# A decoder trunk in split fp32: weight chunks that restart at each output projection, and dummy matmuls at the program's head

## The chip, the cores and the metric

The kernel runs on one core of a Trainium2 chip. Its time is the device time of one execution in microseconds (us): the median of several executions. A core has five engines that each take their instructions strictly in order: TensorE (PE; its weight loads are listed as PEld), VectorE (DVE), ScalarE (ACT), GpSimd (POOL) and SyncE (SP, which here only issues DMAs). An engine waits at an instruction until the semaphores that it needs are set; what stands behind it on the same engine waits too.

## The reference

Two layers work on x, 256 tokens by 2048, all in fp32. In each layer three groups of attention heads share one normalised input; then follows a gated MLP with a short causal convolution.

```
for l in range(DEPTH):                       # DEPTH = 2
    h = _rmsnorm(x, attn_norm[l])
    z = einsum('bsd,de->bse', h, w_in[l])    # 2048 -> 4934, split into q, k, v ... of three kinds of heads
    ...
    x = x + einsum('bsm,md->bsd', mix, w_o[l])           # output projection, 2048 -> 2048
    h = _rmsnorm(x, ffn_norm[l])
    u = conv3(einsum('bsd,df->bsf', h, w_up)) + conv_b   # 2048 -> 2 x 5632, three taps along the tokens
    a, g = split(u, 2)
    x = x + einsum('bsf,fd->bsd', silu(g) * a, w_down)   # 5632 -> 2048
return _rmsnorm(x, final_norm)
```

## The kernel before, in words

**Split arithmetic.** Each fp32 weight block of 128x128 is split on the chip into a high part (`hi`, a cast on ACT, L134) and the rest (`lo`, a subtract on DVE, L135). An activation tile `h` holds its own high and low part side by side, 2 x 256 tokens. A product is hi times both parts (512 columns, L189) plus lo times the high part (256 columns, L194).

**The weight stream.** All weights lie in HBM as one stream of blocks in the order in which PE reads them. SP loads them in chunks of `CH` = 16 blocks, 1 MB, into three `raw` buffers (`load`, L105). `convert` splits a chunk in pieces of `SUB` = 8 blocks: one cast and one subtract of 128x1024 each, into five `hi` and five `lo` buffers. `weights(b)` is asked for each block in turn; at the first block of a piece it converts that piece and the two behind it, and loads the next two chunks. So the place of the casts and subtracts among the other work follows from where a piece begins.

**Where pieces begin.** A layer's stream has 708 blocks up to the output projection and 2368 from there (output projection and MLP). Before, chunks are counted over the whole stream. 708 is 44 x 16 + 4, so in layer 0 everything from the output projection on lies 4 blocks, half a piece, off the pieces, and so does layer 1's attention; in layer 1 the second 708 makes it 8, a whole piece, and its output projection and MLP lie on whole pieces.

**Tiles.** `mm_t` makes one tile of 128 outputs out of 16 blocks: two whole pieces, or three pieces with a half at each end. Tiles alternate in order (`turn_of`): one has its 16 high matmuls (L189), then its 16 low ones (L194); the next has one high, 16 low, 15 high. `mm_t2` (L225 to L228) makes the first two tiles of a stage together, step by step of the inner loop, and `mm_first` (L207 to L211) the next; `mm_v` (L243 to L245) serves the output and down projections.

**The MLP.** A half of it makes 22 pairs of tiles, then a down projection with them. The first pair is an `mm_t2`, and 21 pairs of `mm_t` follow in the first half, 22 in the second. Each tile leaves its PSUM bank (there are three, tag `mm`) through `total`: an ACT copy of the upper half (L252) and a DVE sum (L254). Then POOL multiplies by the row norm (L817), ACT takes the tap with the bias (L820), DVE the two other taps (L821, L822). For the second tile of a pair ACT computes the Silu (L824), POOL the product (L825), and ACT and DVE the high and low part of the result (L503, L504).

**What sets the order.** The program is written in the order of the loops, with other work in background generators; a scheduler of the Tile framework then fixes each engine's order when the program is built. Nothing is decided on the chip.

**Start and end.** Before the first weights arrive, 18 dummy matmuls of 128x512 on a zeroed tile `heat` (L272) are issued into a bank that nobody reads; in the built program they stand in the middle of the first `mm_t2`, after ten of the 16 steps of its inner loop. `warm` is a small tile of zeros; in the last down projection, `gain(2)` (L844) calls `activation(warm, warm, Sqrt)`, and after the last matmul `norm.cols` (L434 to L436) takes the final root.

Of the kernel before, what the change touches and what calls it, by code (L numbers as in the profile page):

```python
# [15 lines left out]
P = 128  # L16
D = 2048
T = 256
KT = D // P
# [35 lines left out]
BIG = _split12(2.0 * math.pi * 4096.0, 4)  # L55


@with_exitstack
def kernel(ctx: ExitStack, tc: tile.TileContext, xin, xnat, pos, wstream, cst, par, fin, out):
    nc = tc.nc  # L60
# [29 lines left out]
    def f(ap):  # L90
        return ap.bitcast(F32)

    nblk = wstream.shape[0]
    wflat = wstream.rearrange("b p f -> (b p f)")
    nch = (nblk + CH - 1) // CH
    raws, subs = {}, {}
    bounds = [(i, min(SUB, nblk - i)) for i in range(0, nblk, SUB)]
    sub_of = {b: s for s, (at, n) in enumerate(bounds) for b in range(at, at + n)}

    def load(c):  # L100
        if c >= nch or c in raws:
            return
        n = min(CH, nblk - c * CH)
        t = wpool.tile([P, CH * P], F32, tag="raw", name=nm("raw"), bufs=3)
        nc.sync.dma_start(  # L105
            t[:, : n * P], wflat[c * CH * P * P : (c * CH + n) * P * P].rearrange("(p e) -> p e", p=P)
        )
        raws[c] = t

    def load_first():  # L110
# [10 lines left out]
    def convert(s, between=None):  # L121
        if s >= len(bounds) or s in subs:
            return
        at, n = bounds[s]
        c = at // CH
        load(c)
        o = (at - c * CH) * P
        src = raws[c][:, o : o + n * P]
        hi = wpool.tile([P, SUB * P], F32R, tag="hi", name=nm("hi"), bufs=5)
        lo = wpool.tile([P, SUB * P], F32R, tag="lo", name=nm("lo"), bufs=5)  # L130
        step = SUB // 2 * P if c < 3 else SUB * P
        for o in range(0, n * P, step):
            a = slice(o, min(o + step, n * P))
            nc.scalar.copy(hi[:, a], src[:, a])  # L134
            nc.vector.tensor_tensor(lo[:, a], src[:, a], f(hi[:, a]), ALU.subtract)  # L135
            if between is not None:
                between()
        subs[s] = (hi, lo)

    def weights(b, n=1):  # L140
        s = sub_of[b]
        at = bounds[s][0]
        if b == at:
            convert(s)
            convert(s + 1)
            convert(s + 2)
            load(b // CH + 1)
            load(b // CH + 2)
        o = (b - at) * P
        hi, lo = subs[s]  # L150
        return hi[:, o : o + n * P], lo[:, o : o + n * P]

# [107 lines left out]
    xr = [big.tile([P, D], F32, tag=f"x{t}", name=f"x{t}") for t in range(2)]  # L260
    xg = [slot().rearrange("p (j t) -> p j t", j=2) for k in range(KT // 2)]
    xT = [xg[k // 2][:, k % 2] for k in range(KT)]
    warm = small(4)
    nc.vector.memset(warm, 0.0)
    nc.scalar.activation(warm, warm, AF.Square)
    nc.scalar.dma_start(pr[0][:, :Q_CV], par[0, :, :Q_CV])
    load_first()
    heat = slot(F32R)
    nc.vector.memset(f(heat), 0.0)
    hot = bank("pv", 1)  # L270
    for i in range(18):
        nc.tensor.matmul(hot, heat[:, :P], heat, start=(i == 0), stop=(i == 17))  # L272
    nc.sync.dma_start(cs, cst)
    nc.sync.dma_start(pint, pos)
    nc.sync.dma_start(pr[0][:, Q_CV:], par[0, :, Q_CV:])
# [283 lines left out]
    for l in range(DEPTH):  # L559
# [244 lines left out]
        for half in range(2):  # L804
# [30 lines left out]
            else:  # L835
# [5 lines left out]
                def gain(j):  # L841
                    a = slice(j * 512, (j + 1) * 512)
                    if j == 2:
                        nc.scalar.activation(warm, warm, AF.Sqrt)  # L844
                    for t in range(2):
                        nc.gpsimd.tensor_tensor(xr[t][:, a], xr[t][:, a], gf[j], ALU.mult)

# [20 lines left out]
def _layout(inputs):  # L868
# [62 lines left out]
    flat = stream.reshape(-1)  # L931
    pend = np.concatenate(blocks)
    del blocks[:]
    for c in range(0, nblk, CH):
        n = min(CH, nblk - c)
        flat[c * P * P : (c + n) * P * P].reshape(P, n, P)[:] = pend[c : c + n].transpose(1, 0, 2)
    del pend

# [59 lines left out]
```

## Time and profile before

| | |
|---|---|
| median of 3 runs | 2303.63 us (2303.62 to 2304.62) |
| profiled execution | 2304.31 us, of it 2302.5 in the span of the trace |
| PE busy | 2246.5 us, 98% of the span, 12090 matmuls |
| DVE busy | 1472.0 us, 64% |
| ACT busy | 1205.4 us, 52% |
| POOL busy | 414.5 us, 18% |
| L135 subtracts | 775, 950.3 us, mean 1235 ns |
| L134 casts | 775, 803.9 us, mean 1040 ns |
| HBM traffic | 413.59 MB, 180 GB/s |
| chain that ended last | PE 78%, DVE 11%, ACT 5%, POOL 4%, issue 2% |

How to read it: shares of busy time are averages over the whole program. The span is what lies between the first and the last instruction of the profiled execution; the time has 1.8 us more. The chain follows the work back from the last instruction to what released each step: PE holds 78% of it, so for the rest of the time some other engine was what PE waited for, or what stood at the two ends. Which stage that is, the tables by stretch and the waits of PE tell.

### The profile page before, as it was taken

How to read it: one execution, taken by the hardware profiler on the slowest of the kernel's cores; microseconds unless marked ns; L12 is line 12 of the kernel's file. 1: busy time of each engine (PE TensorE's matmuls, PEld its weight loads, DVE VectorE, ACT ScalarE, POOL GpSimd, SP SyncE). 2: the span in 40 equal slices, each digit the busy share in tenths (PEclk: the TensorE clock that was granted, in tenths of full speed). 3: DMA queues.
4: the chain of work that ended last, by engine and by line, in shares of the span. 5: the costliest groups of instructions: out<-in, count | busy, mean ns of one | idle time of the engine just before them, and what ended most of it. 6: DMA issues, size and time to landing. Idle time of an engine off the chain costs nothing.

```text
span 2302.5 us, 31046 instructions
## 1 busy us (share of the span) xinstructions
PE 2246.5 (98%) x12090; PEld 1934.1 (84%) x12090; DVE 1472.0 (64%) x2316; ACT 1205.4 (52%) x1866; POOL 414.5 (18%) x395
## 2 busy tenths in 40 slices
PE   8999999999999999999999999999999999999997
PEld 7888978888778887787888988888888888888886
DVE  7767866666664566666565577666666645777653
ACT  6455645554553445555454566456555534555543
POOL 4600000222210022221014001002433201222210
PEclk9999999999999999999999999999999999999999
DMA  8544435444455544545545444354555555555653
GB/s 301 193 158 163 155 137 185 163 174 167 166 198 200 184 166 166 181 165 195 189 166 206 161 163 165 128 183 174 191 184 183 202 200 184 193 191 183 213 189 119
DMA packets 60771, 413.59 MB, mean 180 GB/s; under 512 B 6864, under 2 KB 6992, under 8 KB 11600
## 3 DMA queue, kind: packets, MB, share of 16 engines
q1 hardware_dynamic: 59904, 410.54, 49.8%
q8 instruction: 95, 1.56, 0.3%
q10 hardware_dynamic: 720, 1.07, 0.1%
q14 instruction: 52, 0.43, 0.1%
HBM read 409.49 MB, written 2.10 MB: 179 GB/s over the span
## 4 chain that ended last, share of the span: by engine, by line
PE 78%; DVE 11%; ACT 5%; POOL 4%; issue 2%; DMA 0%; ACTq 0%; POOLq 0%; DVEq 0%; SPq 0%
PE mm L189 23%; PE mm L194 12%; PE mm L243 11%; PE mm L245 11%; PE mm L244 11%; DVE lo L135 6%; POOL tmp L817 2%; ACT tmp L820 2%; POOL tmp L825 2%; ACT hi L134 2%; PE s L466 2%; DVE tmp L821 2%; PE mm L228 1%; DVE tmp L254 1%; DVE tmp L822 1%
## 5 line engine op out<-in xcount | busy, mean ns | idle before, releaser
L135 DVE TENSOR_TENSOR lo<-raw,hi 128x1024 fp32r<-128x1024 f32 (+1 forms) x775 | 950.3, 1235 | 443.5 <-ACT hi L134 399.9
L134 ACT CAST hi<-raw 128x1024 fp32r<-128x1024 f32 (+1 forms) x775 | 803.9, 1040 | 477.0 <-PE mm L245 363.7
L189 PE MATMUL mm<-h,hi 128*128 128x512 f32 x3584 | 862.5, 392 | 0.0
L189 PEld LDWEIGHTS mm<-h,hi 128*128 128x128 f32 x3584 | 664.8, 188 | 134.1 <-ACT tmp L252 1.3
L194 PEld LDWEIGHTS mm<-h,lo 128*128 128x128 f32 x3584 | 462.2, 190 | 51.6 <-DVE lo L135 38.0
L194 PE MATMUL mm<-h,lo 128*128 128x256 f32 x3584 | 473.7, 284 | 31.4 <-DVE lo L135 31.4
L243 PE MATMUL mm<-hi,slot 128*128 128x512 f32 x992 | 388.7, 392 | 4.6 <-DVE tmp L254 4.6
L245 PE MATMUL mm<-hi,slot 128*128 128x512 f32 x992 | 385.5, 389 | 0.0
L244 PE MATMUL mm<-lo,slot 128*128 128x512 f32 x992 | 385.4, 388 | 0.0
L817 POOL TENSOR_TENSOR tmp<-tmp,rstd 128x256 f32<-128x256 f32 x176 | 188.7, 1072 | 1078.1 <-DVE tmp L254 923.4
L820 ACT ACTIVATE tmp<-tmp,par 128x256 f32<-128x256 f32 x176 | 105.9, 602 | 355.1 <-POOL tmp L817 355.1
L243 PEld LDWEIGHTS mm<-hi,slot 128*128 128x128 f32 x992 | 186.7, 188 | 46.7 <-DVE tmp L254 5.5
L821 DVE SCALAR_TENSOR_TENSOR tmp<-tmp,par,tmp 128x255 f32<-128x255 f32 x176 | 85.0, 483 | 212.8 <-ACT tmp L820 212.7
L245 PEld LDWEIGHTS mm<-hi,slot 128*128 128x128 f32 x992 | 186.7, 188 | 38.7
L244 PEld LDWEIGHTS mm<-lo,slot 128*128 128x128 f32 x992 | 186.7, 188 | 37.0
L825 POOL TENSOR_TENSOR tmp<-tmp,tmp 128x256 f32<-128x256 f32 x88 | 93.4, 1062 | 205.3 <-ACT tmp L824 205.3
L252 ACT COPY tmp<-mm 128x256 f32<-128x256 f32 (+1 forms) x233 | 85.1, 365 | 51.9 <-PE mm L194 24.9
L254 DVE TENSOR_TENSOR tmp<-mm,tmp 128x256 f32<-128x256 f32 (+1 forms) x233 | 97.4, 418 | 0.6 <-ACT tmp L252 0.5
L822 DVE SCALAR_TENSOR_TENSOR tmp<-tmp,par,tmp 128x254 f32<-128x254 f32 x176 | 85.1, 483 | 6.2
L504 DVE TENSOR_TENSOR slot<-tmp,slot 128x256 fp32r<-128x256 f32 x96 | 40.6, 423 | 72.6 <-ACT slot L503 72.6
L503 ACT CAST slot<-tmp 128x256 fp32r<-128x256 f32 x96 | 39.0, 406 | 67.2 <-POOL tmp L825 65.6
L243 PE MATMUL mm<-hi,h 128*128 128x512 f32 (+1 forms) x192 | 68.3, 356 | 0.0
(192 smaller groups left out, 1501.3 us busy)
## 6 DMA issues: line engine op xcount, KB each, us to landing
raw<-in_w SPq DMA_DIRECT2D x381, 1024.0 KB, 4.8
raw<-in_w SPq DMA_DIRECT2D x12, 256.0 KB, 5.4
slot<-in_x SPq DMA_DIRECT2D x8, 256.0 KB, 5.2
x<-in_xn SPq DMA_DIRECT2D x2, 1024.0 KB, 10.9
slot<-in_fin SPq DMA_DIRECT2D x4, 256.0 KB, 6.6
out<-x SPq DMA_DIRECT2D x4, 256.0 KB, 3.7
out<-x ACTq DMA_DIRECT2D x4, 256.0 KB, 3.8
raw<-in_w SPq DMA_DIRECT2D x1, 512.0 KB, 3.2
```

Source lines behind the costliest of these rows:

```text
L134: nc.scalar.copy(hi[:, a], src[:, a])
L135: nc.vector.tensor_tensor(lo[:, a], src[:, a], f(hi[:, a]), ALU.subtract)
L189: nc.tensor.matmul(ps, ws[i][0], moving[i], start=(i == 0), stop=bool(flip and i == k - 1))
L194: nc.tensor.matmul(ps[:, :T], ws[i][1], moving[i][:, :T], start=False, stop=(not flip and i == k - 1))
L243: nc.tensor.matmul(ps[t][:, :n], s_hi, hi, start=(i == 0), stop=False)
L244: nc.tensor.matmul(ps[t][:, :n], s_hi, lo, start=False, stop=False)
L245: nc.tensor.matmul(ps[t][:, :n], s_lo, hi, start=False, stop=(i == k - 1))
L254: nc.vector.tensor_tensor(u[:rows], ps[:rows, :T], t[:rows], ALU.add)
L817: nc.gpsimd.tensor_tensor(uu, u, rstd, ALU.mult)
L820: nc.scalar.activation(y, uu, AF.Identity, scale=q_[:, w + 2 : w + 3], bias=q_[:, w + 3 : w + 4])
L821: nc.vector.scalar_tensor_tensor(y[:, 1:], uu[:, : T - 1], q_[:, w + 1 : w + 2], y[:, 1:], ALU.mult, ALU.add)
L825: nc.gpsimd.tensor_tensor(ys[0], ys[0], ys[1], ALU.mult)
```

## The change

It does three things. `chunk_list` cuts the stream anew at each output projection (and at each layer's start), so that a layer has 45 + 148 chunks, the 45th with 4 blocks; every tile then lies on whole pieces. All in all there are 386 chunks in place of 385, and 770 pieces in place of 769. The layout on the host follows the same list. Second, the dummy matmuls are 11, not 18, and are written ahead of all else. Third, the early root in `gain(2)` takes the sums of squares of the second quarter as its operand, not the zeros of `warm`.

```diff
--- before.py
+++ after.py
@@ -55,6 +55,14 @@
 BIG = _split12(2.0 * math.pi * 4096.0, 4)
 
 
+def chunk_list():
+    out, at = [], 0
+    for n in (KT * 39 + 84, 16 * KT + 3 * FT * KT) * DEPTH:
+        out += [(at + i, min(CH, n - i)) for i in range(0, n, CH)]
+        at += n
+    return out
+
+
 @with_exitstack
 def tile_trunk_kernel(ctx: ExitStack, tc: tile.TileContext, xin, xnat, pos, wstream, cst, par, fin, out):
     nc = tc.nc
@@ -90,21 +98,19 @@
     def f(ap):
         return ap.bitcast(F32)
 
-    nblk = wstream.shape[0]
     wflat = wstream.rearrange("b p f -> (b p f)")
-    nch = (nblk + CH - 1) // CH
+    chunks = chunk_list()
+    nch = len(chunks)
     raws, subs = {}, {}
-    bounds = [(i, min(SUB, nblk - i)) for i in range(0, nblk, SUB)]
-    sub_of = {b: s for s, (at, n) in enumerate(bounds) for b in range(at, at + n)}
+    bounds = [(c, i, min(SUB, n - i)) for c, (at, n) in enumerate(chunks) for i in range(0, n, SUB)]
+    sub_of = {chunks[c][0] + o + i: (s, i) for s, (c, o, n) in enumerate(bounds) for i in range(n)}
 
     def load(c):
         if c >= nch or c in raws:
             return
-        n = min(CH, nblk - c * CH)
+        at, n = chunks[c]
         t = wpool.tile([P, CH * P], F32, tag="raw", name=nm("raw"), bufs=3)
-        nc.sync.dma_start(
-            t[:, : n * P], wflat[c * CH * P * P : (c * CH + n) * P * P].rearrange("(p e) -> p e", p=P)
-        )
+        nc.sync.dma_start(t[:, : n * P], wflat[at * P * P : (at + n) * P * P].rearrange("(p e) -> p e", p=P))
         raws[c] = t
 
     def load_first():
@@ -121,10 +127,9 @@
     def convert(s, between=None):
         if s >= len(bounds) or s in subs:
             return
-        at, n = bounds[s]
-        c = at // CH
+        c, o, n = bounds[s]
         load(c)
-        o = (at - c * CH) * P
+        o = o * P
         src = raws[c][:, o : o + n * P]
         hi = wpool.tile([P, SUB * P], F32R, tag="hi", name=nm("hi"), bufs=5)
         lo = wpool.tile([P, SUB * P], F32R, tag="lo", name=nm("lo"), bufs=5)
@@ -138,15 +143,14 @@
         subs[s] = (hi, lo)
 
     def weights(b, n=1):
-        s = sub_of[b]
-        at = bounds[s][0]
-        if b == at:
+        s, o = sub_of[b]
+        if o == 0:
             convert(s)
             convert(s + 1)
             convert(s + 2)
-            load(b // CH + 1)
-            load(b // CH + 2)
-        o = (b - at) * P
+            load(bounds[s][0] + 1)
+            load(bounds[s][0] + 2)
+        o *= P
         hi, lo = subs[s]
         return hi[:, o : o + n * P], lo[:, o : o + n * P]
 
@@ -260,16 +264,16 @@
     xr = [big.tile([P, D], F32, tag=f"x{t}", name=f"x{t}") for t in range(2)]
     xg = [slot().rearrange("p (j t) -> p j t", j=2) for k in range(KT // 2)]
     xT = [xg[k // 2][:, k % 2] for k in range(KT)]
+    heat = slot(F32R)
+    nc.vector.memset(f(heat), 0.0)
+    hot = bank("pv", 1)
+    for i in range(11):
+        nc.tensor.matmul(hot, heat[:, :P], heat, start=(i == 0), stop=(i == 10))
     warm = small(4)
     nc.vector.memset(warm, 0.0)
     nc.scalar.activation(warm, warm, AF.Square)
     nc.scalar.dma_start(pr[0][:, :Q_CV], par[0, :, :Q_CV])
     load_first()
-    heat = slot(F32R)
-    nc.vector.memset(f(heat), 0.0)
-    hot = bank("pv", 1)
-    for i in range(18):
-        nc.tensor.matmul(hot, heat[:, :P], heat, start=(i == 0), stop=(i == 17))
     nc.sync.dma_start(cs, cst)
     nc.sync.dma_start(pint, pos)
     nc.sync.dma_start(pr[0][:, Q_CV:], par[0, :, Q_CV:])
@@ -841,7 +845,7 @@
                 def gain(j):
                     a = slice(j * 512, (j + 1) * 512)
                     if j == 2:
-                        nc.scalar.activation(warm, warm, AF.Sqrt)
+                        nc.scalar.activation(warm[:, :2], norm.sums[:, :, 1], AF.Sqrt)
                     for t in range(2):
                         nc.gpsimd.tensor_tensor(xr[t][:, a], xr[t][:, a], gf[j], ALU.mult)
 
@@ -931,8 +935,7 @@
     flat = stream.reshape(-1)
     pend = np.concatenate(blocks)
     del blocks[:]
-    for c in range(0, nblk, CH):
-        n = min(CH, nblk - c)
+    for c, n in chunk_list():
         flat[c * P * P : (c + n) * P * P].reshape(P, n, P)[:] = pend[c : c + n].transpose(1, 0, 2)
     del pend
 
```

In the changed program lines up to L135 move down by five (L134 is L139, L135 is L140), those behind by four.

**DVE, first half of the MLP in layer 0, one pair of tiles and the start of the next.** `lo`, `raw` and `hi` are the pieces, `mm` a PSUM bank, `tmp` a 128x256 tile between two steps. Before:

```order
L821 SCALAR_TENSOR_TENSOR tmp_5115<-tmp_5113,par_73,tmp_5115 128x255
L822 SCALAR_TENSOR_TENSOR tmp_5115<-tmp_5113,par_73,tmp_5115 128x254
L135 TENSOR_TENSOR lo_5179<-raw_5075,hi_5178 128x1024
L135 TENSOR_TENSOR lo_5183<-raw_5128,hi_5182 128x1024
L254 TENSOR_TENSOR tmp_5164<-mm_5119,tmp_5162 128x256
L821 SCALAR_TENSOR_TENSOR tmp_5168<-tmp_5166,par_73,tmp_5168 128x255
L822 SCALAR_TENSOR_TENSOR tmp_5168<-tmp_5166,par_73,tmp_5168 128x254
L135 TENSOR_TENSOR lo_5232<-raw_5128,hi_5231 128x1024
L504 TENSOR_TENSOR slot_5174<-tmp_5115,slot_5174 128x256
L135 TENSOR_TENSOR lo_5236<-raw_5186,hi_5235 128x1024
L254 TENSOR_TENSOR tmp_5222<-mm_5177,tmp_5220 128x256
```

And with the change:

```order
L825 SCALAR_TENSOR_TENSOR tmp_5108<-tmp_5106,par_73,tmp_5108 128x255
L826 SCALAR_TENSOR_TENSOR tmp_5108<-tmp_5106,par_73,tmp_5108 128x254
L140 TENSOR_TENSOR lo_5178<-raw_5117,hi_5177 128x1024
L140 TENSOR_TENSOR lo_5225<-raw_5175,hi_5224 128x1024
L258 TENSOR_TENSOR tmp_5157<-mm_5112,tmp_5155 128x256
L825 SCALAR_TENSOR_TENSOR tmp_5161<-tmp_5159,par_73,tmp_5161 128x255
L826 SCALAR_TENSOR_TENSOR tmp_5161<-tmp_5159,par_73,tmp_5161 128x254
L140 TENSOR_TENSOR lo_5231<-raw_5175,hi_5230 128x1024
L508 TENSOR_TENSOR slot_5167<-tmp_5108,slot_5167 128x256
L258 TENSOR_TENSOR tmp_5215<-mm_5170,tmp_5213 128x256
L140 TENSOR_TENSOR lo_5283<-raw_5228,hi_5282 128x1024
```

The last two rows have changed places: the sum (L254, now L258) stands ahead of the subtract that it stood behind. On ACT the copy L252 likewise stands ahead of that piece's cast. In layer 1's MLP the order is the same in both programs.

**PE, start of the program.** `pv` is the bank of the dummies, `mm` the two banks of the first `mm_t2`. Before:

```order
L226 MATMUL mm_215<-h_149,lo_185 128x256
L228 MATMUL mm_215<-h_149,hi_184 128x512
L272 MATMUL pv_116<-slot_114 128x512 x18
L226 MATMUL mm_214<-h_150,lo_185 128x256
L228 MATMUL mm_214<-h_150,hi_184 128x512
L226 MATMUL mm_215<-h_150,lo_185 128x256
```

And with the change:

```order
L996 UNCONDITIONAL_BRANCH
L271 MATMUL pv_89<-slot_87 128x512 x11
L229 MATMUL mm_207<-h_133,hi_149 128x512
L230 MATMUL mm_207<-h_133,lo_150 128x256
L229 MATMUL mm_208<-h_133,hi_149 128x512
L230 MATMUL mm_208<-h_133,lo_150 128x256
```

The block has moved from the middle of the first pair of tiles to the head of PE's program. Farther on, the small matmuls that spread the first row norm stand ahead of the third tile; before they stood behind its first steps.

**ACT, end of the program.** `rcol` is the column of the final root, `sums` the sums of squares. Before:

```order
L416 ACTIVATE slot_20565,sums_19794<-x_77 128x512
L416 ACTIVATE slot_20568,sums_19794<-x_78 128x512
L435 ACT_TABLE_LOAD
L435 ACTIVATE rcol_20570<-rcol_20570,cs 128x2
L860 ACTIVATE x_78<-x_78,rcol_20570 128x512 x2
```

And with the change:

```order
L139 CAST hi_20523<-raw_20477 128x1024
L420 ACTIVATE slot_20564,sums_19793<-x_77 128x512
L420 ACTIVATE slot_20567,sums_19793<-x_78 128x512
L439 ACTIVATE rcol_20569<-rcol_20569,cs 128x2
L864 ACTIVATE x_78<-x_78,rcol_20569 128x512 x2
```

The table load ahead of the last root is gone from there; it stands with the early root (now L848), behind the squares of the second quarter and well ahead of the last casts. Before, the scheduler had put the early root, which waited for nothing, at the start of the program.

## Rows read from the trace of the kernel before

**Rows 1.** Waits of PE: who waited for whom, us in total, times, longest
```profile
PE mm L194 <- DVE lo L135: 31.4, 32, 1.0
PE mm L225 <- DVE h L390: 6.7, 1, 6.7
PE mm L243 <- DVE tmp L254: 4.6, 2, 2.3
PE pv L498 <- ACT slot L493: 1.2, 1, 1.2
```

**Rows 2.** Stretches: us; busy of PE, PEld, DVE, ACT, POOL; PEclk; DMA share; GB/s
```profile
408.27:661.60 253.33, 237.79 (x1348) 207.59 (x1346) 158.10 (x228) 131.33 (x207) 55.98 (x63) 1.00 0.48 170
783.91:1048.64 264.73, 248.86 (x1409) 217.37 (x1408) 164.30 (x234) 134.11 (x210) 55.31 (x63) 1.00 0.48 171
1571.41:1805.73 234.32, 234.32 (x1347) 206.76 (x1346) 157.76 (x230) 133.70 (x211) 90.56 (x63) 1.00 0.52 186
1925.41:2170.78 245.37, 245.37 (x1409) 216.51 (x1408) 177.03 (x240) 143.21 (x216) 66.45 (x64) 1.00 0.53 189
```

**Rows 3.** Timeline, layer 0: start, us, engine, line, operation, [idle before <- releaser]
```profile
511.35 0.42 ACT L824 ACTIVATE tmp<-tmp 128x256 f32<-128x256 f32 x1 [0.19 <-DVE tmp L822]
...
513.36 1.05 ACT L134 CAST hi<-raw 128x1024 fp32r<-128x1024 f32 x1
...
514.44 1.23 DVE L135 TENSOR_TENSOR lo<-raw,hi 128x1024 fp32r<-128x1024 f32 x1 [0.53 <-ACT hi L134]
...
515.59 0.42 DVE L254 TENSOR_TENSOR tmp<-mm,tmp 128x256 f32<-128x256 f32 x1
...
516.08 0.73 POOL L817 TENSOR_TENSOR tmp<-tmp,rstd 128x256 f32<-128x256 f32 x1 [3.06 <-DVE tmp L254]
...
516.85 0.60 ACT L820 ACTIVATE tmp<-tmp,par 128x256 f32<-128x256 f32 x1 [1.23 <-POOL tmp L817]
...
523.75 0.42 ACT L824 ACTIVATE tmp<-tmp 128x256 f32<-128x256 f32 x1 [0.19 <-DVE tmp L822]
```

**Rows 4.** Timeline, layer 1, the same place of a pair
```profile
1701.50 0.42 ACT L824 ACTIVATE tmp<-tmp 128x256 f32<-128x256 f32 x1 [0.20 <-DVE tmp L822]
...
1701.82 1.04 ACT L134 CAST hi<-raw 128x1024 fp32r<-128x1024 f32 x1
...
1703.63 0.43 DVE L504 TENSOR_TENSOR slot<-tmp,slot 128x256 fp32r<-128x256 f32 x1 [1.07 <-ACT slot L503]
1703.98 0.42 DVE L254 TENSOR_TENSOR tmp<-mm,tmp 128x256 f32<-128x256 f32 x1
1704.31 1.22 DVE L135 TENSOR_TENSOR lo<-raw,hi 128x1024 fp32r<-128x1024 f32 x1
1704.47 1.65 POOL L817 TENSOR_TENSOR tmp<-tmp,rstd 128x256 f32<-128x256 f32 x1 [1.31 <-DVE tmp L254]
...
1706.15 0.60 ACT L820 ACTIVATE tmp<-tmp,par 128x256 f32<-128x256 f32 x1 [2.28 <-POOL tmp L817]
```

**Rows 5.** Table by stretch, behind layer 0's second wait of L243 (columns as rows 2)
```profile
1052.00:1056.00 4.00, 4.00 (x12) 3.13 (x13) 2.72 (x4) 2.75 (x4) 0.58 (x1) 0.60 0.07 29
```

**Rows 6.** Timeline, start of the program
```profile
16.09 4.26 PE L272 MATMUL pv<-slot 128*128 128x512 f32 x18
...
17.08 0.88 DVE L390 SCALAR_TENSOR_TENSOR h<-slot,par,h 128x256 fp32r<-128x256 f32 x2
...
20.88 4.28 DVE L542 TENSOR_TENSOR slot<-slot,slot 128x512 f32<-128x512 f32 x5
...
24.43 0.39 PE L207 MATMUL mm<-h,hi 128*128 128x512 f32 x1
...
37.34 3.92 PE L189 MATMUL mm<-h,hi 128*128 128x512 f32 x16
```

**Rows 7.** Timeline, end of the program
```profile
2292.12 1.28 ACT L435 ACT_TABLE_LOAD   x1
2292.14 0.16 DVE L434 TENSOR_REDUCE rcol<-sums 128x2 f32<-128x8 f32 x1 [0.79 <-ACT slot L416]
```

## The prediction

> **What bounds the kernel now.** I read the waits of TensorE (PE) first, then tables by stage, then a few microseconds of timeline. PE is busy nearly all the time, so only its waits and its idle moments can be won. The waits [rows 1] are few, and one group holds most: 32 times an L194 matmul (low half of a weight times the activations) waited for the L135 subtract that makes that low half, 31.4 us in all. Two L243 matmuls, the first of a down projection, waited for an L254 sum, 4.6 us.
>
> The reader should then see where these waits lie. Rows 2 cut out the four halves of the two feed-forward stages (FFN), from the first up matmul (L189) of a half to the first L243. Layer 0's halves take 253.33 and 264.73 us, layer 1's 234.32 and 245.37 us with the same matmuls; in layer 1 PE is busy for the whole of each stretch. So layer 0 loses 19.0 and 19.4 us. The two layers compute the same; what differs is where their tiles lie in the weight pieces (layer 0: half a piece off; layer 1's FFN: on whole pieces), and so the order in which the subtracts stand among the other work.
>
> Next, one steady pair of layer 0 [rows 3]: from one L824 to the next 12.40 us pass (511.35 to 523.75). A half has 21 or 22 such pairs, and 234.32 / 21 = 11.16 us is what PE alone needs for one. So in layer 0 the bound is not PE but a ring through ACT, DVE and GpSimd (POOL): each engine takes its instructions in order, and each waits for another's result. PE lives on a lead at first: 21 x 1.24 = 26.0 us would be lost without one, 19.0 were, so the lead was worth about 7 us.
>
> **The change, part by part.**
>
> *FFN of layer 0.* On whole pieces the order on DVE becomes: subtract, L504, L254, subtract; before it was subtract, L504, subtract, L254. So L254, which feeds the POOL multiply L817 and through it the tap L820, no longer stands behind a subtract that waits for its own cast L134. I walk the ring again, from L824 on.
> - Now [rows 3]: L824 to L820 is 511.35 to 516.85, 5.50 us; L820 to the next L824 is 6.90 us.
> - After, the first part: L824 to the cast 0.32 (1701.50 to 1701.82, where the neighbours are the same [rows 4]); cast to subtract 1.08, subtract to its follower on DVE 1.15 (513.36, 514.44, 515.59 [rows 3]); L504 to L254 0.35 (1703.63 to 1703.98 [rows 4]); L254 to L820 2.17 (1703.98 to 1706.15 [rows 4]). Sum 5.07 us.
> - The second part keeps its order, hence 6.90 us. The ring is 11.97 us.
>
> The price that decides is the 2.17. It holds an L817 of 1.65 us, whereas the one in rows 3 takes 0.73. In rows 4 a subtract starts at 1704.31, just before L817 at 1704.47, and L817 ends 0.59 us after that subtract does; in rows 3 no subtract runs beside it. POOL's multiply is held back while such a subtract runs. In the new order a subtract follows L254 at once, as in rows 4, so I take the held price.
>
> The Trainium skill says the same of these two operations (SBUF — State Buffer, "Who interferes with whom"): a DVE instruction with two SBUF inputs contends with a GpSimd instruction that reads SBUF, and whoever issues first has the shared port pair for its whole instruction. The trace agrees, 1.65 against 0.73 us. By that rule an L817 that came first would run free, and this is the first rival below.
>
> A ring of 11.97 is still above PE's 11.16, so waits remain: 0.81 us a pair. With the same lead, 21 x 0.81 - 7 = 10.0 us, and for the other half 22 x 0.81 - 7.9 = 9.9 us. Of 38.4 us 19.9 stay, **-18.5 us**. Each handover may be off by a few hundredths; with 0.1 us on the ring that is 4.3 us either way.
>
> *Down projections of layer 0.* The 4.6 us of rows 1: L254 will come 4.24 - 2.90 = 1.34 us earlier behind L824 (515.59 less 511.35, against the first four steps above), but PE, which now waits for the last subtract in that row and later for the one before, resumes earlier too. I take **0**, with all 4.6 gone as the lower end. Behind the second wait PE, which had stood still for 2.3 us, has a granted clock of 0.60 over 4 us [rows 5], that is, it runs at the lower of its two levels for most of them; 0.4 x 4 = 1.6 us are lost. I take them as staying, since the wait stays, and their end for the lower bound.
>
> *Dummies.* Eighteen now stand between real matmuls and occupy PE from 16.09 for 4.26 us, 0.24 each [rows 6]. After, eleven stand first, and the first real matmul cannot start before 6.7 us, when the first activations are split (the L225 wait [rows 1]); that hides eleven even at twice their duration (5.2 us). Without the block, the opening pair of tiles is bound by its last splits, which end at 17.96 (17.08 + 0.88 [rows 6]). Behind the block six steps of the pair's inner loop are left (16.09 + 4.26 to 24.43: 4.1, about 0.7 each); one such step behind 17.96, with a little for the handover, puts the next tile at 18.8 instead of 24.43: 5.6 us. Not all arrives. The sum of squares on DVE ends at 25.16 whatever PE does (20.88 + 4.28 [rows 6]), and the small matmuls that read it now stand ahead of the third tile, not inside it. The tile before it has 16 half-steps of 0.35, so it is through at 18.8 + 5.6 = 24.4, and PE then waits 0.7 us. **-4.9 us**: the first ordinary tile starts at about 32.4 instead of 37.34 [rows 6]. Ends: -5.6, and 0 if something else (weights, a cast) is then late.
>
> *Table load at the end.* ACT loads the square-root table on the last path, 1.28 us from 2292.12 [rows 7]. The new operand ties the earlier use to sums made inside the last down projection, so the load falls where ACT has room and PE is the bound. The root then waits only for the reduction, which ends at 2292.30 (2292.14 + 0.16 [rows 7]) and not for the load, which ends at 2293.40: **-1.1 us** (0 to -1.3). The new early root on the start's path costs a load where ACT waits for PE's small matmuls in any case: 0.
>
> *Attention and the rest.* Layer 1's attention comes onto whole pieces; its only PE wait is 1.2 us [rows 1], which may go or not: 0, end -1.2. Two short chunks instead of one, one more piece: one cast and one subtract of half the length or less, and DMA works half the time in these stretches [rows 2]: 0.
>
> **Sum:** -18.5 - 4.9 - 1.1 = -24.5 on the profiled 2304.31, so 2279.8. The median is 0.7 below the profiled execution: **2279 us**.
>
> **Rivals.**
> 1. *All of the FFN loss goes.* If L817 starts before the subtract (in rows 4 two starts 0.16 us apart decide it) it takes 0.73, the ring shrinks by 0.92 to 11.05, below PE's 11.16, and layer 0 runs like layer 1: -38.4, then also the down projections' -4.6 and the dip's -1.6, -4.9 and -1.1: 2254. For it: 0.16 us is little. Against: rows 4 show the same neighbours, and there L817 is the one held; layer 1 runs without waits all the same, since its order spreads the subtracts otherwise. 0.12.
> 2. *The FFN stays as it is.* The ring keeps 12.40, since another wait takes the place of the moved one: 2304.3 - 4.9 - 1.1 = 2298. That would be the change not doing what it says. For it: the same casts and subtracts remain. Against: the moved step is on the ring itself [rows 3]. 0.07.
> 3. *Slower.* Both L817 of a pair are held, the second by a subtract too: 11.97 + 0.92 = 12.89, 0.49 over now, times 43 pairs +21, less 6: 2319. It decides from a ring of 12.40 + 6 / 43 = 12.54 on. Against: behind the second L254 DVE's next instruction is L821, which waits for that very L817, so no subtract can start beside it. 0.04.
>
> **How the numbers follow.** The forecast has 0.77. Its own range is 2267 to 2288: the ring's 4.3 both ways, the dummies' end above, the down projections and the dip below. The 8-in-10 range goes a little further to both rivals, for halves that differ: 2261 to 2290. A measurement of this kernel tells 0.2%, 4.6 us, from no change. Rival 2 is just past it, and may fall within if the start gives less: of its 0.07 half counts as the same. Faster 0.92, same 0.04, slower 0.04.
>
> **What would show it.** Right: waits of the low matmuls for subtracts still there, some 25 of 0.7 to 0.8 us, only in layer 0; its halves at about 243 and 255 us; L817 there alternating between 0.73 and 1.65; the first ordinary tile near 32 us; no table load behind the last matmul. Wrong: halves like layer 1's (rival 1), or unchanged with a new releaser in the waits (rival 2), or every L817 at 1.65 (rival 3).

## The result, and the profile after

The changed kernel takes 2279.58 us (median of 4 runs, 2278.24 to 2280.38) where the kernel before takes 2303.62: a ratio of 0.9894, 95% interval 0.9877 to 0.9912. 24.0 us are saved; 2279 was forecast. The profiled execution has 2280.38 us, its span 2278.2, 24.3 less than before.

Cut at the same places of the program, the two spans compare as follows. The cuts are the first ordinary tile, the first L189 (now L193) of each half of the MLP and the first L243 (now L247) of each down projection.

| stretch | before | after | difference | forecast |
|---|---|---|---|---|
| up to the first ordinary tile | 37.34 | 32.37 | -4.97 | -4.9 |
| layer 0, rest of attention and first MLP pair | 370.93 | 371.16 | +0.23 | 0 |
| layer 0, MLP first half | 253.33 | 245.94 | -7.39 | -9.0 |
| its down projection | 122.31 | 123.40 | +1.09 | 0 |
| MLP second half | 264.73 | 255.81 | -8.92 | -9.5 |
| its down projection, layer 1 up to its MLP | 522.77 | 519.32 | -3.45 | 0 |
| layer 1, MLP with its first down projection | 599.37 | 599.37 | 0.00 | 0 |
| last down projection and end | 131.72 | 130.83 | -0.89 | -1.1 |
| sum | 2302.5 | 2278.2 | -24.3 | -24.5 |

The waits of PE after, against [rows 1]:

```profile
PE mm L198 <- DVE lo L140: 15.8, 27, 0.6
PE mm L247 <- DVE tmp L258: 3.5, 2, 1.8
PE misc L358 <- DVE slot L546: 0.5, 1, 0.5
```

The low matmuls still wait for subtracts, 27 times, but for 0.6 us at most where it was 1.0. All of these waits are in layer 0's MLP, as the table by stretch shows (columns as [rows 2]):

```profile
403.53:649.47 245.94, 237.66 (x1347) 207.55 (x1346) 155.78 (x227) 129.65 (x208) 64.21 (x63) 1.00 0.50 176
772.87:1028.68 255.81, 248.28 (x1410) 217.19 (x1408) 161.54 (x233) 132.75 (x211) 64.28 (x63) 1.00 0.51 177
653.00:657.00 4.00, 4.00 (x12) 3.10 (x11) 2.70 (x5) 2.75 (x4) 0.75 (x1) 0.57 0.55 223
1031.00:1035.00 4.00, 3.71 (x16) 3.10 (x17) 2.70 (x5) 2.00 (x3) 1.65 (x1) 1.00 0.76 262
```

The waits add up to 15.8 us, while the two halves lose 22.0 against layer 1's 234.32 and 245.37 us. The rest is not listed as waits but stands in PE's busy time, which is 3.3 and 2.9 us above layer 1's (237.66 and 248.28). So a wait costs about 0.2 us more than its row says, and 27 times the ring's 0.80 us, worked out below, are 21.6.

The last two rows stand behind the waits of L247 at the start of the two down projections. The granted clock falls behind the first wait now and not behind the second; before it fell behind the second [rows 5]. That is worth some 1.6 us in either place.

One steady pair of layer 0 in the changed kernel (timeline; start, length, engine, line, operation, idle time before and what ended it), to set beside [rows 3]:

```profile
493.16 0.42 ACT L828 ACTIVATE tmp<-tmp 128x256 f32<-128x256 f32 x1 [1.13 <-DVE tmp L826]
493.48 1.04 ACT L139 CAST hi<-raw 128x1024 fp32r<-128x1024 f32 x1
...
494.55 1.23 DVE L140 TENSOR_TENSOR lo<-raw,hi 128x1024 fp32r<-128x1024 f32 x1 [1.49 <-ACT hi L139]
...
495.69 0.42 DVE L508 TENSOR_TENSOR slot<-tmp,slot 128x256 fp32r<-128x256 f32 x1
495.83 1.22 PE L198 MATMUL mm<-h,lo 128*128 128x256 f32 x8 [0.59 <-DVE lo L140]
496.03 0.42 DVE L258 TENSOR_TENSOR tmp<-mm,tmp 128x256 f32<-128x256 f32 x1
496.36 1.22 DVE L140 TENSOR_TENSOR lo<-raw,hi 128x1024 fp32r<-128x1024 f32 x1
496.52 1.65 POOL L821 TENSOR_TENSOR tmp<-tmp,rstd 128x256 f32<-128x256 f32 x1 [2.13 <-DVE tmp L258]
...
498.21 0.60 ACT L824 ACTIVATE tmp<-tmp,par 128x256 f32<-128x256 f32 x1 [2.16 <-POOL tmp L821]
...
502.62 0.73 POOL L821 TENSOR_TENSOR tmp<-tmp,rstd 128x256 f32<-128x256 f32 x1 [4.45 <-DVE tmp L258]
...
505.12 0.42 ACT L828 ACTIVATE tmp<-tmp 128x256 f32<-128x256 f32 x1 [1.13 <-DVE tmp L826]
```

The ring (from one instruction to its next occurrence a pair later), here L828 to L828, is 505.12 - 493.16 = 11.96 us. Its first part, up to the tap L824, is 498.21 - 493.16 = 5.05. The sum L258 now stands ahead of the subtract; POOL's multiply L821 starts 0.16 us after that subtract and takes 1.65 us. The other multiply of the pair, with no subtract beside it, takes 0.73.

The start and the end of the changed program (timeline), to set beside [rows 6, 7]:

```profile
1.45 4.39 PE L271 MATMUL pv<-slot 128*128 128x512 f32 x11 [1.45 <-DVE small L273]
6.68 0.50 PE L229 MATMUL mm<-h,hi 128*128 128x512 f32 x1 [0.83 <-DVE h L394]
...
19.02 0.40 PE L211 MATMUL mm<-h,hi 128*128 128x512 f32 x1
...
32.37 3.92 PE L193 MATMUL mm<-h,hi 128*128 128x512 f32 x16
...
2268.73 0.16 DVE L438 TENSOR_REDUCE rcol<-sums 128x2 f32<-128x8 f32 x1 [0.79 <-ACT slot L420]
2268.92 0.30 ACT L439 ACTIVATE rcol<-rcol,cs 128x2 f32<-128x2 f32 x1 [0.23 <-DVE rcol L438]
```

Eleven dummies are over before the first activations are split. The next tile begins at 19.02 in place of 24.43, the first ordinary one at 32.37. At the end the root follows the reduction directly.

### The profile page after: what moved, and what is told of

The parts are those of the page before. It is cut to its first block, busy times and chain, and to the rows that moved or that the text cites. A ratio compares the mean times of both kernels' runs of the same rounds, so it can differ in the third digit from the quotient of the medians.

```text
span 2278.2 us, 31040 instructions
## 1 busy us (share of the span) xinstructions
PE 2244.7 (99%) x12083; PEld 1931.5 (85%) x12083; DVE 1468.5 (64%) x2317; ACT 1198.6 (53%) x1867; POOL 436.6 (19%) x395
## 4 chain that ended last, share of the span: by engine, by line
PE 84%; DVE 6%; ACT 5%; issue 3%; POOL 2%; DMA 0%; SPq 0%; ACTq 0%; POOLq 0%; DVEq 0%
PE mm L193 27%; PE mm L198 15%; PE mm L247 12%; PE mm L249 11%; PE mm L248 11%; DVE lo L140 4%; ACT hi L139 3%; PE s L470 2%; POOL tmp L821 2%; ACT tmp L824 1%; PE mm L232 1%; DVE tmp L825 1%; DVE tmp L826 1%; ACT tmp L828 1%; PE mm L763 1%
## 5 line engine op out<-in xcount | busy, mean ns | idle before, releaser
L140 DVE TENSOR_TENSOR lo<-raw,hi 128x1024 fp32r<-128x1024 f32 (+1 forms) x776 | 952.3, 1236 | 496.4 <-ACT hi L139 457.0
L139 ACT CAST hi<-raw 128x1024 fp32r<-128x1024 f32 (+1 forms) x776 | 799.3, 1039 | 469.1 <-PE mm L249 364.4
L193 PE MATMUL mm<-h,hi 128*128 128x512 f32 x3584 | 862.8, 392 | 0.0
L193 PEld LDWEIGHTS mm<-h,hi 128*128 128x128 f32 x3584 | 664.8, 188 | 134.5 <-ACT tmp L256 1.3
L198 PE MATMUL mm<-h,lo 128*128 128x256 f32 x3584 | 472.7, 284 | 15.8 <-DVE lo L140 15.8
L821 POOL TENSOR_TENSOR tmp<-tmp,rstd 128x256 f32<-128x256 f32 x176 | 224.3, 1274 | 1041.7 <-DVE tmp L258 731.7
L247 PE MATMUL mm<-hi,slot 128*128 128x512 f32 x992 | 388.8, 392 | 3.5 <-DVE tmp L258 3.5
L824 ACT ACTIVATE tmp<-tmp,par 128x256 f32<-128x256 f32 x176 | 105.9, 602 | 357.3 <-POOL tmp L821 357.1
L247 PEld LDWEIGHTS mm<-hi,slot 128*128 128x128 f32 x992 | 186.6, 188 | 46.1 <-DVE tmp L258 4.4
L829 POOL TENSOR_TENSOR tmp<-tmp,tmp 128x256 f32<-128x256 f32 x88 | 76.0, 863 | 208.8 <-ACT tmp L828 208.8
L258 DVE TENSOR_TENSOR tmp<-mm,tmp 128x256 f32<-128x256 f32 (+1 forms) x233 | 97.3, 417 | 4.3 <-ACT tmp L256 4.1
L826 DVE SCALAR_TENSOR_TENSOR tmp<-tmp,par,tmp 128x254 f32<-128x254 f32 x176 | 85.0, 483 | 6.2
L828 ACT ACTIVATE tmp<-tmp 128x256 f32<-128x256 f32 x88 | 36.8, 418 | 61.5 <-DVE tmp L826 61.4
L247 PE MATMUL mm<-hi,h 128*128 128x512 f32 (+1 forms) x192 | 68.3, 356 | 0.0
L249 PE MATMUL mm<-hi,h 128*128 128x512 f32 (+1 forms) x192 | 67.9, 354 | 0.0
```

What stands on the lines that cost most here:

```text
L193: nc.tensor.matmul(ps, ws[i][0], moving[i], start=(i == 0), stop=bool(flip and i == k - 1))
L198: nc.tensor.matmul(ps[:, :T], ws[i][1], moving[i][:, :T], start=False, stop=(not flip and i == k - 1))
L247: nc.tensor.matmul(ps[t][:, :n], s_hi, hi, start=(i == 0), stop=False)
L249: nc.tensor.matmul(ps[t][:, :n], s_lo, hi, start=False, stop=(i == k - 1))
L258: nc.vector.tensor_tensor(u[:rows], ps[:rows, :T], t[:rows], ALU.add)
L821: nc.gpsimd.tensor_tensor(uu, u, rstd, ALU.mult)
```

## The experiments

Ten kernels ran, in three groups; the kernel before ran with each group, with medians from 2304.3 to 2305.5. Ratios are to that, with 95% intervals.

**1. The chunk list alone.** The changed kernel with the dummies and the early root of the kernel before.

> Only the new chunk list; dummies and early root as before. Theory (the ring of layer 0's MLP, and what it does downstream, is separate from start and end): the parts add, so this takes layer 0's MLP halves from 253.3 and 264.7 us to about 246 and 256 and saves 18.7 of the 23.9 us that the whole change saved in the profiled executions: 2285 to 2286 us. Rival (the dummies at the head give a lead that the MLP lives on): the halves stay above 250 and 260 us, and the time is over 2290.

Measured: 2286.28 us, 0.9917 (0.9902 to 0.9932). The halves take 246.15 and 256.11 us; 27 waits for subtracts. As expected: the MLP's gain owes nothing to the start.

**2. Start and root alone.** The kernel before with eleven dummies at the head and the new operand.

> Only the dummies (eleven, at the head) and the new operand of the early root; chunks as before. Theory: first ordinary tile at about 32.4 us, 4.7 us saved at the start of the MLP, 0.9 to 1.1 at the end: 2298 to 2299 us; the 32 waits of layer 0's low matmuls stay at about 31 us. Rival: a start that comes earlier is eaten by layer 0's attention or MLP: 2302 to 2303.

Measured: 2300.11 us, 0.9977 (0.9968 to 0.9986), 4.9 us less, where 4.7 at the start and 0.9 to 1.1 at the end, together 2298 to 2299, had been expected. In its trace PE's clock falls behind both waits in front of layer 0's down projections (granted 0.57 over 661 to 665 and over 1050 to 1054 us), in the kernel before behind one, which is some 1.6 us more; the first ordinary tile is at 32.64, the halves are 253.62 and 265.01 us, with 32 waits of 32.1 us in all. The two parts add up: 18.7 and 4.9 us make 23.6, against 24.0 for the whole.

**3. and 4. The kinds of tiles.** More than half of the loss in layer 0's halves was left (22.0 of 38.4 us), though all tiles lay on whole pieces as in layer 1. The two layers' MLPs still differ in one thing that can be seen in the program: the two kinds of tiles alternate through the whole program, and layer 0's pairs begin with the kind "1 high, 16 low, 15 high", layer 1's with "16 high, 16 low". So the kinds were changed places, in layer 0 alone, and in layer 1 alone:

```diff
+        if l == 0:            # second kernel: l == 1, and turn_of[0] = 1
+            turn_of[0] = 0
         for half in range(2):
...
             elif l < DEPTH - 1:
+                turn_of[0] = 1        # first kernel only: layer 1 stays as it was
```

> The changed kernel, but in layer 0's MLP the two kinds of tiles change places in each pair (first tile 16 high then 16 low, second tile 1 high, 16 low, 15 high), as they stand in layer 1. Theory (what is left of layer 0's loss is the order in which the scheduler sets the subtracts about the sum, and that order follows from the kinds): DVE's order becomes that of layer 1, the halves become 234.3 and 245.4 us, no waits for subtracts, no wait in front of the down projections, no dip behind it: 2280.4 - 11.6 - 10.4 - 3.7 - 1.8 = 2253 us. Rival (something else in layer 0 is slower: late data, less room): 2275 to 2281 us.

> The changed kernel, but in layer 1's MLP the two kinds change places, as they stand in layer 0. Everything is on whole pieces still. Theory (kinds set the order, order sets the ring): layer 1's halves become about 246 and 256 us with some 27 more waits of low matmuls for subtracts, and each of its down projections begins with a wait of about 1.75 us: 2280.4 + 22 + 3.7 + 3.4 = 2309 us, slower than the kernel before. Rival (whole pieces are enough, layer 1 is safe): 2279 to 2282 us.

Measured: 2252.27 us, 0.9772 (0.9757 to 0.9786), and 2310.25 us, 1.0023 (1.0012 to 1.0033). Both as expected. In the first kernel layer 0's halves take 234.31 and 245.37 us, what layer 1's take, and PE has no wait in either MLP. In the second, layer 1 loses what layer 0 loses; waits of PE:

```profile
PE mm L198 <- DVE lo L140: 33.1, 54, 0.9
PE mm L247 <- DVE tmp L258: 7.1, 4, 1.8
```

The first kernel's pair in layer 0 (timeline) corrects the picture of the prediction:

```profile
498.92 1.03 ACT L139 CAST hi<-raw 128x1024 fp32r<-128x1024 f32 x1
...
499.98 1.23 DVE L140 TENSOR_TENSOR lo<-raw,hi 128x1024 fp32r<-128x1024 f32 x1
500.14 0.42 ACT L830 ACTIVATE tmp<-tmp 128x256 f32<-128x256 f32 x1 [0.19 <-DVE tmp L828]
...
502.28 0.43 DVE L508 TENSOR_TENSOR slot<-tmp,slot 128x256 fp32r<-128x256 f32 x1 [1.07 <-ACT slot L507]
...
502.95 1.22 DVE L140 TENSOR_TENSOR lo<-raw,hi 128x1024 fp32r<-128x1024 f32 x1
503.12 1.65 POOL L823 TENSOR_TENSOR tmp<-tmp,rstd 128x256 f32<-128x256 f32 x1 [1.31 <-DVE tmp L258]
...
507.86 1.22 DVE L140 TENSOR_TENSOR lo<-raw,hi 128x1024 fp32r<-128x1024 f32 x1
508.09 1.58 POOL L823 TENSOR_TENSOR tmp<-tmp,rstd 128x256 f32<-128x256 f32 x1 [3.32 <-DVE tmp L258]
...
511.44 0.42 ACT L830 ACTIVATE tmp<-tmp 128x256 f32<-128x256 f32 x1 [0.19 <-DVE tmp L828]
```

This pair is from the first half. Both multiplies are held back (1.65 and 1.58 us), and still nothing waits. The ring is 511.44 - 500.14 = 11.30 us, longer than PE's 11.16: 21 x 0.14 = 2.9 us in this half, which the lead covers. In the second half it is not longer than what PE needs: there only one multiply of a pair is held (1.65 and 0.74 us), and from Silu to Silu 11.14 us pass (timeline):

```profile
873.49 0.42 ACT L830 ACTIVATE tmp<-tmp 128x256 f32<-128x256 f32 x1 [0.51 <-DVE tmp L828]
...
884.63 0.42 ACT L830 ACTIVATE tmp<-tmp 128x256 f32<-128x256 f32 x1 [0.50 <-DVE tmp L828]
```

In this order a cast and its subtract, which in the changed kernel stand behind the Silu (493.48 and 494.55), start ahead of it (498.92 and 499.98), so L508 follows 2.14 us behind the Silu (502.28 - 500.14), not 2.53 (495.69 - 493.16), and the sum with it.

**5. Kinds changed, chunks as before.** The same edit in the kernel before.

> The kernel before, with the kinds of layer 0's MLP changed places and nothing else; its tiles lie half a piece off. Theory (kinds help only where tiles lie on whole pieces, since here VectorE's order stays subtract, L504, subtract, L254): 32 waits of about 1 us stay, 2302 to 2306 us. Rival (kinds alone decide, the chunks never mattered): layer 0 runs like layer 1, about 2260 us.

Measured: 2278.88 us, 0.9887 (0.9872 to 0.9901). This expectation fell: neither side had it. Waits of PE and one pair of layer 0 (timeline):

```profile
PE mm L194 <- DVE lo L135: 4.6, 21, 0.2
```

```profile
492.59 1.03 ACT L134 CAST hi<-raw 128x1024 fp32r<-128x1024 f32 x1
...
493.64 1.22 DVE L135 TENSOR_TENSOR lo<-raw,hi 128x1024 fp32r<-128x1024 f32 x1
493.81 0.42 ACT L826 ACTIVATE tmp<-tmp 128x256 f32<-128x256 f32 x1 [0.19 <-DVE tmp L824]
...
496.27 1.22 DVE L135 TENSOR_TENSOR lo<-raw,hi 128x1024 fp32r<-128x1024 f32 x1
497.41 0.42 DVE L254 TENSOR_TENSOR tmp<-mm,tmp 128x256 f32<-128x256 f32 x1
...
505.59 0.42 ACT L826 ACTIVATE tmp<-tmp 128x256 f32<-128x256 f32 x1 [0.19 <-DVE tmp L824]
```

DVE's order is indeed the old one, with the sum behind the subtract. But on ACT a cast has moved ahead of the Silu (L826), so the subtract at 496.27 finds its cast (492.59) done; in [rows 3] it stood idle for 0.53 us until the cast ended. The sum comes 3.60 us behind the Silu, not 4.24 (497.41 - 493.81 and 515.59 - 511.35), and the ring is 11.78 us, not 12.40. I had compared DVE's order alone. Kinds alone save 25.4 us, chunks alone 18.7; with start and end (4.9) that makes 49.0, and both kinds and chunks, with that start and end, saved 52.7. In the halves alone the two take away 25.3 and 15.8 of the 38.4 us. The rows show them at different steps of the ring: kinds end the subtract's wait for its cast, chunks move the sum ahead of that subtract. Neither alone ends the two waits in front of layer 0's down projections (4.3 us are left with kinds alone, 3.5 with chunks alone); both together do.

**6. and 7. The multiply by the row norm on VectorE.** In layer 0 alone `nc.vector.tensor_tensor` takes the place of `nc.gpsimd.tensor_tensor` in L821. Run 6 does so for both tiles of a pair; VectorE then does it right behind the sum, ahead of the subtract.

> The changed kernel; in layer 0's MLP alone the multiply by the row norm goes from GpSimd to VectorE, where it stands right behind the sum and ahead of the subtract; kinds and chunks as in the changed kernel. Theory (the sum to tap step of 2.16 us, which holds a GpSimd multiply held back by a subtract, keeps the ring at 11.96 us): a multiply on VectorE takes about 0.42 us and can't be held, sum to tap is some 0.8 us, both times in a pair; ring 11.96 - 1.35 - 0.5 = 10.1 us, below TensorE's 11.16; all 27 waits and both waits of the down projections go: about 2253 us. Rival (VectorE, which gets two more instructions a pair, becomes the bound, or the ring is closed by the casts and subtracts alone): waits stay, 2270 us or more.

Measured: 2251.95 us, 0.9772 (0.9755 to 0.9788); halves of 234.26 and 245.32 us, no waits in the MLP. With kinds as in the changed kernel, taking the step out of GpSimd's hands is enough where it also comes to stand ahead of the subtract; run 7a shows what is left when it stands behind.

Run 7 does it for one tile at a time, 7a for the first tile, 7b for the second:

> As norm_on_dve, but of the two row-norm multiplies of a pair only the held one (first tile's, 1.65 us) goes to VectorE; the scheduler sets it behind the subtract. Theory (it doesn't matter whether a GpSimd multiply is held until the subtract ends or a VectorE one is queued behind it): sum to tap 0.33 + 1.15 + 0.42 + 0.07 = 1.97 us in place of 2.16, ring 11.96 - 0.19 = 11.77; with leads of 5.2 and 7.2 us a half loses 21 x 0.61 - 5.2 = 7.6 and 22 x 0.61 - 7.2 = 6.2 us; with the two waits of the down projections and a dip 2252.3 + 13.8 + 3.5 + 1.6 = 2271 us. Rival (GpSimd itself is the slow one): 2260 us or less.

> The counterpart: only the free multiply of a pair (second tile's, 0.74 us) goes to VectorE, the held one stays on GpSimd. Theory (a ring and a lead): sum to tap 0.8 in place of 1.33 us, ring 11.96 - 0.52 = 11.44; a half loses 21 x 0.28 - 5.2 = 0.7 and 22 x 0.28 - 7.2 = 0 us; the held one stays at 1.65 us in the trace; with what is left of the down projections' waits 2253 to 2259 us. Rival (the held multiply alone is the cause of the waits): 2272 to 2280 us.

Measured for the first tile (7a): 2266.28 us, 0.9831 (0.9813 to 0.9849), halves of 238.89 and 250.68 us. From one Silu of layer 0 to the next (timeline):

```profile
489.44 0.42 ACT L828 ACTIVATE tmp<-tmp 128x256 f32<-128x256 f32 x1 [1.13 <-DVE tmp L826]
...
492.30 0.42 DVE L258 TENSOR_TENSOR tmp<-mm,tmp 128x256 f32<-128x256 f32 x1
...
493.77 0.42 DVE L821 TENSOR_TENSOR tmp<-tmp,rstd 128x256 f32<-128x256 f32 x1
494.23 0.60 ACT L824 ACTIVATE tmp<-tmp,par 128x256 f32<-128x256 f32 x1 [0.94 <-DVE tmp L821]
...
501.12 0.42 ACT L828 ACTIVATE tmp<-tmp 128x256 f32<-128x256 f32 x1 [1.13 <-DVE tmp L826]
```

The ring, 11.68 us, is 0.09 us shorter than worked out and the halves lose 4.6 and 5.3 in place of 7.6 and 6.2. The clock, for whose fall 1.6 us had been added, did not fall behind either down projection's wait. From sum to tap 1.93 us pass (494.23 - 492.30), 1.97 worked out: that a multiply queued on VectorE behind the subtract costs nearly what a held one costs on GpSimd is borne out. Measured for the second tile (7b): 2251.97 us, 0.9769 (0.9753 to 0.9784), nothing lost. The time is a little below what was expected, but the held multiply did not stay. In this order it starts first (timeline of layer 0):

```profile
489.41 0.74 POOL L821 TENSOR_TENSOR tmp<-tmp,rstd 128x256 f32<-128x256 f32 x1 [1.31 <-DVE tmp L258]
...
489.79 1.44 DVE L140 TENSOR_TENSOR lo<-raw,hi 128x1024 fp32r<-128x1024 f32 x1 [0.46 <-ACT hi L139]
```

It takes 0.74 us, and the subtract that comes 0.38 us later takes 1.44 in place of 1.22. So this run doesn't tell which of the two multiplies mattered; it shows that the order of the starts decides which engine is held.

**8. The subtract in two halves.** Layer 0's subtracts of 128x1024 become two of 128x512 each.

> The changed kernel; layer 0's MLP subtracts each piece in two instructions of 128x512, so what can hold a GpSimd multiply back is half as long (and the scheduler sets sums between halves). Theory A (the hold lasts as long as one VectorE instruction and GpSimd gets in between two): the held multiply takes about 1.1 us in place of 1.65, the ring shrinks by some 0.5 us, 2263 to 2270 us. Theory B (back to back subtracts keep GpSimd out): the multiply takes 1.65 us or more, 2279 to 2283 us. If nothing holds it and it is slow for another reason, it stays at 1.65 exactly.

Measured: 2254.14 us, 0.9781 (0.9767 to 0.9796). One pair of layer 0 (timeline):

```profile
500.13 0.42 ACT L831 ACTIVATE tmp<-tmp 128x256 f32<-128x256 f32 x1 [1.13 <-DVE tmp L829]
...
503.40 0.68 DVE L141 TENSOR_TENSOR lo<-raw,hi 128x512 fp32r<-128x512 f32 x1
503.56 1.12 POOL L824 TENSOR_TENSOR tmp<-tmp,rstd 128x256 f32<-128x256 f32 x1 [2.20 <-DVE tmp L261]
...
504.00 1.23 DVE L143 TENSOR_TENSOR lo<-raw,hi 128x512 fp32r<-128x512 f32 x1
...
511.48 0.42 ACT L831 ACTIVATE tmp<-tmp 128x256 f32<-128x256 f32 x1 [1.13 <-DVE tmp L829]
```

GpSimd's multiply is held by the first half only and ends 0.60 us after it (504.68 against 504.08); the second half, which takes 0.68 us alone, is then held in its turn and takes 1.23. That is theory A's mechanism. The time is below its range of 2263 to 2270 us: the ring is 11.35 us (511.48 - 500.13), 0.61 shorter and not 0.5, since the scheduler also set the sum of the other tile half a piece earlier, and its 21 x 0.19 = 4.0 us are covered by the lead. The range was also too high by its own ring: at 11.46, 21 x 0.30 less the lead of 5.2 us is 1.1 us. What is left is a wait of 1.3 us in front of the first down projection; less these 1.3 us the time would be about 2252.8 us (an estimate), near runs 3 and 6.

**9. No dummies.** The kernel of run 3 without any dummy matmul.

> The kernel of the run kinds_layer0 without any dummy matmul. Theory (the start was won by taking eighteen dummies out of the first tiles; that eleven at the head keep the clock up is worth little): the first matmuls run at the lower clock as in the kernel before, the opening pair ends at about 20.2 us in place of 19.0, and 0.5 us of that is hidden in the wait for the sum of squares: +0.6 us, 2252.9. Rival 1 (the head dummies are worth most of the 4.9 us): 2255 to 2257. Rival 2 (splits alone set the pace): 2252.3.

Measured: 2252.66 us, 0.9775 (0.976 to 0.9789), where run 3 has 0.9772: no difference that these runs can tell. The first matmuls are in fact slower, 14 in the first 4 us in place of 22, and the next tile begins at 19.85 (19.45 in run 3). But in run 3 the small matmuls wait 0.6 us for the sum of squares behind that tile, and here they don't; the first ordinary tile begins at 32.47, in run 3 at 32.72.

## Why the prediction was right, point by point

**The MLP.** The mechanism of the change was right: the moved sum, the held multiply, a ring still above PE's pace. The ring came out at 11.96 us (11.97 forecast), its first part at 5.05 (5.07). The term was -18.5 and measured -16.3. The mis-sized step is the lead: "with the same lead" 10.0 and 9.9 us were to remain, and 11.6 and 10.4 did, 27 waits in place of some 25. (They are 0.6 us long and not 0.7 to 0.8, since the rest of each pair's 0.80 us stands in PE's busy time. The halves "at about 243 and 255" don't follow from the prediction's own terms, which give 244.3 and 255.3; 245.94 and 255.81 came.) By 21 x 0.80 - 11.6 and 22 x 0.80 - 10.4 the lead is 5.2 and 7.2 us in the new order, not 7.0 and 7.9; runs 5 and 7a give 6 to 7. Part of the difference in the first half shows at its beginning: the first Silu and the second are 9.60 us apart there (411.83 and 421.43), 8.44 in the kernel before (416.11 and 424.55). Why the lead differs from order to order no run tells; it is a remainder, not a measured quantity.

**The down projections.** "I take 0" was right in sum and wrong in its parts: the two waits fell from 2.3 to 1.75 us each, and the loss of clock moved from behind the second wait to behind the first. Behind the first, +1.09 us are the clock (1.6) less the shorter wait (0.6). Behind the second, -3.45 us are the shorter wait (0.6), the clock (1.6) and the 1.2 us wait of [rows 1] in layer 1's attention, which went and which I had left standing as a bound.

**Start and end.** -4.9 forecast, -4.97 measured; the small matmuls waited 0.5 us for the sum of squares where 0.7 had been worked out. That it fits to a tenth is luck: over the kernels with the new start the first ordinary tile begins anywhere from 31.92 to 32.72 us, over the three with the old one from 36.62 to 37.91. -1.1 at the end came out as -0.89. The root itself did as forecast. Before, it stood behind the load (timeline of the kernel before):

```profile
2293.42 0.30 ACT L435 ACTIVATE rcol<-rcol,cs 128x2 f32<-128x2 f32 x1
```

It started 1.28 us after the reduction's start (2293.42 - 2292.14 [rows 7]), and now it starts 0.19 after (2268.92 - 2268.73). The missing 0.2 us lies behind the root: from there to the end of the span 9.1 us passed before and 9.3 now.

**The sum** hit because two errors cancelled: the MLP gave 2.2 us less, the stretches taken at 0 gave 2.1 more (+0.23 + 1.09 - 3.45). The number was closer than its parts, by luck.

**The rivals.** None came: the subtract started first each time here. But the first rival's event, a multiply that starts first and runs free, was seen in run 7b, and there the first rival's outcome came too: 2251.97 us, where it said 2254. Its condition, a ring below PE's 11.16, is stricter than needed, though: in the first half of layer 1, which loses nothing, the ring is 11.30 in both kernels, and runs 3 and 8 show that a ring of 11.30 or 11.35 loses nothing in a half. What decides is the ring's excess times the pairs, against the lead:

| kernel | ring, us | lost in the two halves, us |
|---|---|---|
| before | 12.40 | 19.0, 19.4 |
| after | 11.96 | 11.6, 10.4 |
| 5, kinds alone | 11.78 | 6.1, 7.0 |
| 7a, first tile's multiply on VectorE | 11.68 | 4.6, 5.3 |
| 8, subtract in halves | 11.35 | 0.1, 0.0 |
| 3, kinds and chunks | 11.30, then 11.15 | 0.0, 0.0 |

What the prediction had wrong is its sentence that the two layers differ in where their tiles lie in the pieces: alignment was only a part of the difference, and the kinds of tiles were the other part. Layer 1 held both, and comparing the two layers alone could not separate them. The runs with kinds changed did. Run 3, which these runs can't tell from 6 and 7b in time, is two assignments away from the changed kernel and 51 to 53 us faster than the kernel before.

## What to carry to other kernels

Where an engine with the most work still waits, take one steady repetition from the timeline and walk the ring of the other engines from one instruction to its next occurrence: its length, less the busy engine's own pace, times the repetitions, less the lead, is the loss. If two stages with the same work run at different rates, list everything in which they differ (here alignment and the alternation of two kinds) and change one at a time; and compare the order on every engine of the ring, not on one. A step that two engines dispute can be made cheaper by moving it, by halving what holds it, or by an order in which the lead covers it; these three (runs 6, 8 and 3) came to within 2.2 us of each other here (2251.95, 2254.14 and 2252.27).

## What the runs showed of the hardware

GpSimd's multiply and VectorE's subtract, both with two operands in SBUF, hold each other back, whichever starts first: the multiply takes 0.73 us alone, 1.65 beside a subtract of 1.22 that started 0.16 us earlier, 1.12 beside one of 0.68; a subtract of 0.68 us behind a multiply already waiting takes 1.23, and one of 1.22 that starts 0.38 us after a multiply takes 1.44. The Trainium skill describes this (SBUF — State Buffer, "Who interferes with whom"), as whoever issues first keeping the shared ports for its whole instruction. The order agrees in every one of these rows; the durations agree but for 0.13 to 0.14 us, since a multiply shut out until the subtract's end would take 1.22 - 0.16 + 0.73 = 1.79 us, not 1.65, and a subtract shut out until the multiply's end 0.74 - 0.38 + 1.22 = 1.58, not 1.44. What the rows add is that GpSimd gets in between two subtracts that follow each other directly.

PE's clock fell behind one of two waits of equal length (1.75 us each, granted 0.57 and 1.00 over the 4 us that follow), and in the kernel before, where both waits had 2.3 us, it fell behind the other one. Run 1, with the changed kernel's chunks and waits of 1.8 us but the old start, has its fall behind the second wait (granted 0.58 over 1036 to 1040 us; 1.00 over 658 to 662 behind the first), so the length of the wait alone doesn't decide it. Run 2, with waits of 2.3 us, has it behind both, and run 7a, with waits of 1.5 us, behind neither. No run here tells what else decides it.
